# A transformer step on one core: token sums on VectorE, Strassen's products in another order, and norms moved and shared between ScalarE and VectorE

## The chip, the core and the metric

The kernel runs on one core of one Trainium2 chip. A core has a matrix engine (TensorE, PE in the profile; its weight loads are PEld), a vector engine (VectorE, DVE), a scalar engine (ScalarE, ACT), a general engine (GpSimd, POOL) and a queue that issues transfers (SyncE, SP). Each engine takes its own instructions in order and waits on semaphores for the others. [...] The metric is the time of one execution in microseconds (us) on the device; lower is better.

## The reference, cut to what matters

One layer of a hybrid backbone: a context pass over 128 tokens (`x_prompt`) and a denoising step over 1024 tokens (`x_sample`), width 1024. The change touches its last part, the feed-forward block and the norm behind it, and the place where the first norm hands over to it:

```python
h = x * (1 + sc2) + sh2
ff = jnp.square(jax.nn.relu(h @ w_up)) @ w_down      # 1024 -> 4096 -> 1024
x = layer_norm(ALPHA * x + g2 * ff, ln2_g, ln2_b)    # mean and variance of each token's row

def layer_norm(x, g, b):
    mu = jnp.mean(xf, -1, keepdims=True)
    var = jnp.mean(jnp.square(xf - mu), -1, keepdims=True)
    return ((xf - mu) * lax.rsqrt(var + EPS)) * g + b
```

`sc2`, `sh2` and `g2` come from the conditioning vector and differ between the two groups of tokens. All in float32.

## The kernel before

The 1152 tokens are nine blocks of 128, numbered 0 to 8 (8 is the prompt), in three groups of 384: (0, 1, 2), (3, 4, 5), (6, 7, 8). Every product of 32-bit numbers is made as three matmuls: each operand is split into a rounded part (`hi`, written by ACT, line 72) and the remainder (`lo`, a subtraction on DVE, line 73), and hi x hi, hi x lo and lo x hi are added up in PSUM (`mm3`, or line 1366 for the halves below). Weights come as `raw` tiles of 128 x 1024 by DMA on SP's queue (two such tiles), and are split into `wh` and `wl` (four of each).

The instructions are put in order by a planner of the language, not by the text alone: what stands earlier in the text goes first among what is ready by the planner's own clock, and what is ready can be drawn far ahead of its place. The order that comes out is fixed per engine at build time. Tiles of one tag share a number of slots; a tile that finds none waits until an older one is released.

The first norm (lines 1080 to 1100) takes the blocks in the order 0, 1, 2, 6, 7, 8, 3, 4, 5. Behind it the feed-forward block runs in two parts.

*First 384 tokens* (`T0`). Sixteen rounds, one per 256 of the 4096 inner columns: `up_plain` makes the relu squared of 2 x 128 inner rows, `down_bank` adds their part of the output into six PSUM banks that stay (`dacc`). Beside these rounds `act_forms` makes, for the other 768 tokens, the sums and differences that Strassen's method needs: for each of four slices, four sums hi + lo (line 1119), then four differences (line 1125), each split into hi and lo again. They stand in the rounds as a generator of which `some_forms` takes two steps at a time. After the last round `out0` computes per block g2 x sum + ALPHA x residual, the row's statistics and the norm, and stores it.

*Other 768 tokens* (`T1`, blocks 3 to 8). Again sixteen rounds. `up_halves` makes 256 inner rows for two halves of 384 tokens with seven products instead of eight (line 1366), each of 12 matmuls over 384 columns, on combinations of the weights (`up_forms`: four sums and differences on POOL, line 1283, and seven splits into three slots `uf`) and of the tokens (`acts`). The products are added up in PSUM banks x, y and z in the order

```python
ORDER = ("a11", "s2", "s1", "s3", "s4", "a12", "a22")
BANK = "xyzyzxy"
```

and the four results, (row half, token half) = (1,1), (0,1), (0,0) and (1,0) in that order, pass through `half_out` (relu, square, split). A bank that is added to a second time must have been read before. `down` then adds the round's part of the output: for each of six blocks and two halves of 512 columns six matmuls into one of five `d` banks and one DVE add into `acc` (line 1168). One round of `up_halves` is ahead of `down`.

*End.* Before the last `down`, which takes two rounds at once, `residual` turns `acc` into g2 x acc + ALPHA x residual for all six blocks: a product on POOL (line 1130) and two additions on DVE (line 1135) with the residual's halves loaded into tiles `x` (two slots). In the last `down`, DVE multiplies each bank by g2 (line 1171), adds it (line 1172) and takes the row's statistics (line 1173); `ln_stats` makes mean, variance and 1/sqrt (two small steps on POOL, lines 1050 and 1051); `finish` subtracts the mean on ACT (line 1145), multiplies by 1/sqrt and gain on DVE (line 1146), adds the bias on POOL (line 1147; DVE for the last block, in two halves) and stores.

Of the kernel before, what the change touches and what calls it, by code (L numbers as in the profile page):

```python
# [15 lines left out]
D = 1024  # L16
# [20 lines left out]
def hybrid_step_kernel(  # L37
# [1042 lines left out]
    for i, s in enumerate(SORD):  # L1080
# [4 lines left out]
        for half in range(2):  # L1085
# [5 lines left out]
            mm3(g[:], terms)  # L1091
            cs = slice(512 * half, 512 * half + 512)
# [17 lines left out]
    def act_forms(mk):  # L1110
# [4 lines left out]
        for k in range(4):  # L1115
            full = []
            for nm in ("a11", "s1", "a12", "s4"):
                t = mk([128, TB], "v" + nm)
                nc.gpsimd.tensor_tensor(out=t[:], in0=f(acts[nm][0][:, k, :]), in1=f(acts[nm][1][:, k, :]), op=ALU.add)
                full.append(t)  # L1120
                yield
            b11, b12, b21, b22 = full
            t3 = mk([128, TB], "vs3")
            for dst, x, y, nm in ((t3, b22, b12, "s3"), (b11, b12, b11, "s1"), (b22, b22, b11, "s2"), (b21, b21, b22, "a22")):
                nc.gpsimd.tensor_tensor(out=dst[:], in0=x[:], in1=y[:], op=ALU.subtract)
                split(acts[nm][0][:, k, :], acts[nm][1][:, k, :], dst[:])
                yield

    def residual(mk, acc_s, s, g2):
        nc.gpsimd.tensor_tensor(out=acc_s, in0=acc_s, in1=g2, op=ALU.mult)  # L1130
# [6 lines left out]
    def finish(mk, acc_s, s, l2, mv, rs, n):  # L1137
        out = y_sample[0, 128 * s:128 * s + 128, :] if s < NS else y_prompt[0]
        nmu = mk([128, 1], "nmu", 2)
        nc.vector.tensor_scalar(nmu[:], mv[:, 0:1], -1.0, None, ALU.mult)  # L1140
        w = D // n
        for i in range(n):
            cs = slice(w * i, w * i + w)
            y = acc_s[:, cs]
            nc.scalar.activation(out=y, in_=y, func=AF.Identity, bias=nmu[:])  # L1145
            nc.vector.scalar_tensor_tensor(out=y, in0=y, scalar=rs[:], in1=l2[0][:, cs], op0=ALU.mult, op1=ALU.mult)  # L1146
            (nc.gpsimd if n == 1 else nc.vector).tensor_tensor(out=y, in0=y, in1=l2[1][:, cs], op=ALU.add)
            store(out[:, cs], y)

# [3 lines left out]
    def down(mk, acc, toks, fbs, parts, ws, g2, l2, split_last):  # L1153
        last = g2 is not None
        ws = [(parts[i // 2], i % 2, w) for i, w in enumerate(ws)]
        fin = None
        for i, s in enumerate(toks):
            ts_ = slice(128 * i, 128 * i + 128)
            if last:
                st = mk([128, 2, 6], "bst", 2)  # L1160
            for half in range(2):
                cs = slice(512 * half, 512 * half + 512)
                g = psd.tile([128, 512], F32, tag="d", bufs=5, name="d4")
                mm3(g[:], [((a[0][:, m, ts_], a[1][:, m, ts_]), (w[0][:, 0, cs], w[1][:, 0, cs])) for a, m, w in ws])
                if fbs[0] == 0:
                    nc.vector.tensor_copy(out=acc[:, i, cs], in_=g[:])
                elif not last:
                    nc.vector.tensor_tensor(out=acc[:, i, cs], in0=acc[:, i, cs], in1=g[:], op=ALU.add)  # L1168
                else:
                    tm = mk([128, 512], "x", 2)  # L1170
                    nc.vector.tensor_tensor(out=tm[:], in0=g[:], in1=g2[0 if s < NS else 1][:, cs], op=ALU.mult)  # L1171
                    nc.vector.tensor_tensor(out=acc[:, i, cs], in0=acc[:, i, cs], in1=tm[:], op=ALU.add)  # L1172
                    nc.vector.bn_stats(out=st[:, half, :], in_=acc[:, i, cs])  # L1173
            if last:
                if fin:
                    finish(mk, *fin, 1)
                fin = (acc[:, i, :], s, l2, *ln_stats(st, mk))
        if last:
            finish(mk, *fin, 2 if split_last else 1)
# [12 lines left out]
    def up_plain(fb, each):  # L1192
        w = w_pair(w_up, 256 * fb)
# [46 lines left out]
    def some_forms():  # L1240
        next(forms, None)
        next(forms, None)
# [21 lines left out]
    ORDER = ("a11", "s2", "s1", "s3", "s4", "a12", "a22")  # L1264
    BANK = "xyzyzxy"
# [4 lines left out]
    def up_forms(fb):  # L1270
# [24 lines left out]
        yield form(a11)  # L1295
        yield form(s2)
# [5 lines left out]
        yield form(a12)  # L1302
        yield form(a22)
# [4 lines left out]

    def out0(s):
        y = fft([128, D], "y0", 3)  # L1310
        st = fft([128, 2, 6], "bst", 2)
        for half in range(2):
# [3 lines left out]
            nc.vector.tensor_tensor(out=y[:, cs], in0=dacc[s][half][:], in1=g2a[:, cs], op=ALU.mult)  # L1316
            nc.vector.scalar_tensor_tensor(out=y[:, cs], in0=x1[:], scalar=ALPHA, in1=y[:, cs], op0=ALU.mult, op1=ALU.add)
            nc.vector.bn_stats(out=st[:, half, :], in_=y[:, cs])
        finish(fft, y, s, l2a, *ln_stats(st, fft), 1)
# [4 lines left out]
    down_bank(NFB - 1, nxt, ws[1], out0)  # L1324
    s4f.close()
# [6 lines left out]
    ar = pool(st4, "ar", 1)  # L1332
    acc = ar.tile([128, 6, D], F32, name="acc")

# [4 lines left out]
    
# [6 lines left out]
    def up_halves(pre, a, each):  # L1346
# [3 lines left out]
        def tmp(nm):  # L1350
            u[nm] = ft([128, 512], "x", 2)[:, 0:TB] if nm == "v" else ft([128, TB], nm)[:]
# [5 lines left out]
        for j, nm in enumerate(ORDER):  # L1357
            fresh = BANK[j] not in bank
            if fresh:
                bank[BANK[j]] = (psd.tile([128, 512], F32, tag="z", name="pz") if BANK[j] == "z" else  # L1360
# [109 lines left out]
```

## Time and profile before

| | |
|---|---|
| time, median of 3 runs | 2481.15 us (2478.34 to 2482.4) |
| the profiled execution's own time | 2481.37 us |
| its span in the trace | 2479.6 us |
| first norm with the output product, blocks 0 to 8 | 1545 to 1654 us |
| first 384 tokens | 1654 to 1944 us |
| other 768 tokens | 1944 to 2461 us (last matmul) |
| last matmul to the end | 18.4 us |

The profile is that of one execution. Its views give the busy time of each engine by stretch, groups of equal instructions with count, busy time, mean ns of one and the idle time of their engine just ahead of them, the waits of one engine for another, the chain that ended last, and the instructions in order of time (start, length, engine, line, operation, output and inputs, and in brackets the idle time before with what ended it). `L73` is line 73 of the kernel; a helper such as `split` has one line for all its uses, so its groups go by the names of the tiles. A matmul's end is modelled. PE's granted clock is given as a share of full speed.

### The profile page before, as it was taken

How to read it: one execution, taken by the hardware profiler on the slowest of the kernel's cores; microseconds unless marked ns; L12 is line 12 of the kernel's file. 1: busy time of each engine (PE TensorE's matmuls, PEld its weight loads, DVE VectorE, ACT ScalarE, POOL GpSimd, SP SyncE). 2: the span in 40 equal slices, each digit the busy share in tenths (PEclk: the TensorE clock that was granted, in tenths of full speed). 3: DMA queues.
4: the chain of work that ended last, by engine and by line, in shares of the span. 5: the costliest groups of instructions: out<-in, count | busy, mean ns of one | idle time of the engine just before them, and what ended most of it. 6: DMA issues, size and time to landing. Idle time of an engine off the chain costs nothing. (4 is left out here: it accounts for less than half of the span.)

```text
span 2479.6 us, 35982 instructions
## 1 busy us (share of the span) xinstructions
PE 2371.1 (96%) x13293; PEld 2141.3 (86%) x13293; DVE 1492.7 (60%) x2695; ACT 989.7 (40%) x2100; POOL 481.6 (19%) x632
## 2 busy tenths in 40 slices
PE   7999998999999899899999999998999899999996
PEld 4878887788899899889999999887999799999985
DVE  5645635646654464378787346676444666666678
ACT  3323423534433243166666323124333444444432
POOL 1001100211111010144442000236000422222243
PEclk9999999999999999999999999998999999999998
DMA  8275547445655652520002665333443322222223
GB/s 269 83 203 153 149 116 198 136 126 153 193 160 150 173 154 90 106 69 16 16 16 71 207 187 187 101 127 123 141 129 120 114 77 69 68 69 69 69 82 110
DMA packets 234544, 300.46 MB, mean 121 GB/s; under 512 B 24992, under 2 KB 175600, under 8 KB 234368
## 3 DMA queue, kind: packets, MB, share of 16 engines
q1 hardware_dynamic: 234368, 298.16, 39.9%
q8 instruction: 105, 1.72, 0.3%
q14 instruction: 71, 0.58, 0.1%
HBM read 232.88 MB, written 65.21 MB: 120 GB/s over the span
## 5 line engine op out<-in xcount | busy, mean ns | idle before, releaser
L78 PE MATMUL g<-th,wh 128*128 128x384 f32 x1088 | 373.5, 343 | 8.8 <-DVE fm L248 8.8
L80 PE MATMUL g<-th,wl 128*128 128x384 f32 x1088 | 368.3, 338 | 0.0
L79 PE MATMUL g<-tl,wh 128*128 128x384 f32 x1088 | 366.5, 337 | 0.0
L73 DVE TENSOR_TENSOR wl<-raw,wh 128x1024 fp32r<-128x1024 f32 x180 | 226.5, 1265 | 134.6 <-ACT wh L72 133.8
L72 ACT ACTIVATE wh<-raw 128x1024 fp32r<-128x1024 f32 x180 | 188.9, 1058 | 258.2 <-DMA raw<-in_w_down_dram 90.9
L78 PE MATMUL g<-wh,th 128*128 128x512 f32 x600 | 241.1, 402 | 0.3 <-DVE mmt L266 0.2
L80 PE MATMUL g<-wh,tl 128*128 128x512 f32 x600 | 236.2, 394 | 0.0
L79 PE MATMUL g<-wl,th 128*128 128x512 f32 x600 | 236.0, 394 | 0.3 <-DVE wl L73 0.3
L78 PEld LDWEIGHTS g<-th,wh 128*128 128x128 f32 x1088 | 206.5, 190 | 17.6 <-DVE fm L248 9.1
L79 PEld LDWEIGHTS g<-tl,wh 128*128 128x128 f32 x1088 | 206.4, 190 | 0.1
L80 PEld LDWEIGHTS g<-th,wl 128*128 128x128 f32 x1088 | 206.0, 189 | 0.4 <-issue 0.4
L78 PEld LDWEIGHTS g<-wh,th 128*128 128x128 f32 x600 | 113.2, 189 | 25.7 <-issue 3.8
L80 PEld LDWEIGHTS g<-wh,tl 128*128 128x128 f32 x600 | 113.0, 188 | 23.3
L79 PEld LDWEIGHTS g<-wl,th 128*128 128x128 f32 x600 | 113.2, 189 | 21.2 <-DVE wl L73 1.4
L72 ACT ACTIVATE ph<-t 128x384 fp32r<-128x384 f32 x192 | 90.9, 493 | 70.9 <-PE t L872 70.4
L1168 DVE TENSOR_TENSOR acc<-acc,d 128x512 f32<-128x512 f32 x156 | 101.9, 681 | 28.5 <-PE d L80 28.4
L248 DVE COPY fm<-g 128x384 f32<-128x384 f32 x96 | 53.2, 554 | 101.0 <-PE g L80 100.3
L73 DVE TENSOR_TENSOR pl<-t,ph 128x384 fp32r<-128x384 f32 x192 | 104.7, 548 | 9.1 <-ACT ph L72 7.1
L1283 POOL TENSOR_TENSOR wtl<-raw 128x512 f32<-128x512 f32 x16 | 20.9, 1304 | 438.3 <-PE pa L79 211.3
L872 PE MATMUL t<-ident,pe 128*128 128x128 f32 x576 | 96.1, 276 | 6.2 <-DVE pl L73 5.2
L78 PE MATMUL u<-th,wh 128*128 128x384 f32 x256 | 89.6, 350 | 10.9 <-ACT wh L72 7.2
L80 PE MATMUL u<-th,wl 128*128 128x384 f32 x256 | 89.0, 348 | 1.8 <-DVE wl L73 1.8
(386 smaller groups left out, 6002.8 us busy)
## 6 DMA issues: line engine op xcount, KB each, us to landing
raw<-in_w_up_dram SPq DMA_DIRECT2D x64, 512.0 KB
raw<-in_w_down_dram SPq DMA_DIRECT2D x64, 512.0 KB
raw<-in_w_in_dram SPq DMA_DIRECT2D x44, 512.0 KB
kvt<-kvd SPq DMA_DIRECT2D x64, 257.0 KB
raw<-in_w_mod_dram SPq DMA_DIRECT2D x32, 512.0 KB
kvd<-kvs SPq DMA_DIRECT2D x36, 257.0 KB
uw<-ud SPq DMA_DIRECT2D x72, 128.0 KB
bs<-st SPq DMA_DIRECT2D x32, 258.0 KB
```

The costliest lines, as they stand in the source:

```text
L72: nc.scalar.activation(out=hi, in_=src, func=AF.Copy)
L73: nc.vector.tensor_tensor(out=lo, in0=src, in1=f(hi), op=ALU.subtract)
L78: nc.tensor.matmul(out, lhsT=ah, rhs=bh, start=start and i == 0, stop=False)
L79: nc.tensor.matmul(out, lhsT=ah, rhs=bl, start=False, stop=False)
L80: nc.tensor.matmul(out, lhsT=al, rhs=bh, start=False, stop=stop and i == n - 1)
L248: nc.vector.tensor_copy(out=st[:], in_=g[:, 0:TB])
L872: nc.tensor.transpose(pt[:, k, :], pexp[u][:, kt * 128:kt * 128 + 128], ident[:])
L1168: nc.vector.tensor_tensor(out=acc[:, i, cs], in0=acc[:, i, cs], in1=g[:], op=ALU.add)
L1283: nc.gpsimd.tensor_tensor(out=tmp[i], in0=x, in1=y, op=op)
```

## The change

Five things, all behind line 1089:

1. The first weights of `up_plain` are asked for within the last block of the first norm.
2. The token sums and differences of `act_forms`, and the g2 product in `residual` and the bias add in `finish`, are made by DVE instead of POOL. The generator has fewer steps (six per slice instead of eight), and `some_forms` takes one at a time.
3. The seven products run in another order, with four accumulating banks x, y, p and z; `d` has four banks instead of five. The sum for (1,1) moves from POOL to DVE, and (1,0) is made from a22's copy `w`.
4. After the last `down_bank` of the first 384 tokens only g2 x bank is taken; residual, statistics, norm and store follow in the text after the first `up_halves` of the other tokens. The pool of `acc` is opened behind them.
5. At the end two blocks (3 and 4, `LATE`) take their g2 product and residual in the last `down`, behind their banks. Row statistics of all blocks but the last are made by ACT (three passes, two of them with a running sum) with three small steps on POOL; the last block keeps those of DVE.

```diff
@@ first norm @@
             mm3(g[:], terms)
+            if s == SORD[-1] and half == 0:
+                wup0 = w_pair(w_up, 0)
@@ act_forms @@
-            for nm in ("a11", "s1", "a12", "s4"):
+            for i, nm in enumerate(("a11", "s1", "a12", "s4")):
                 t = mk([128, TB], "v" + nm)
-                nc.gpsimd.tensor_tensor(out=t[:], in0=f(acts[nm][0][:, k, :]), in1=f(acts[nm][1][:, k, :]), op=ALU.add)
+                nc.vector.tensor_tensor(out=t[:], in0=f(acts[nm][0][:, k, :]), in1=f(acts[nm][1][:, k, :]), op=ALU.add)
                 full.append(t)
-                yield
+                if i % 2:
+                    yield
...
-                nc.gpsimd.tensor_tensor(out=dst[:], in0=x[:], in1=y[:], op=ALU.subtract)
+                nc.vector.tensor_tensor(out=dst[:], in0=x[:], in1=y[:], op=ALU.subtract)
@@ residual @@
-        nc.gpsimd.tensor_tensor(out=acc_s, in0=acc_s, in1=g2, op=ALU.mult)
+        nc.vector.tensor_tensor(out=acc_s, in0=acc_s, in1=g2, op=ALU.mult)
@@ finish @@
-            nc.scalar.activation(out=y, in_=y, func=AF.Identity, bias=nmu[:])
+            if not centred:
+                nc.scalar.activation(out=y, in_=y, func=AF.Identity, bias=nmu[:])
             nc.vector.scalar_tensor_tensor(out=y, in0=y, scalar=rs[:], in1=l2[0][:, cs], op0=ALU.mult, op1=ALU.mult)
-            (nc.gpsimd if n == 1 else nc.vector).tensor_tensor(out=y, in0=y, in1=l2[1][:, cs], op=ALU.add)
+            nc.vector.tensor_tensor(out=y, in0=y, in1=l2[1][:, cs], op=ALU.add)
...
+    def stats_act(mk, y, jk):
+        sm, nmu, ss, rs = (mk([128, 1], nm, 2) for nm in ("sm", "nmu", "sq", "brs"))
+        nc.scalar.activation(out=jk, in_=y, func=AF.Copy, accum_out=sm[:])
+        nc.gpsimd.tensor_scalar(nmu[:], sm[:], -1.0 / D, None, ALU.mult)
+        nc.scalar.activation(out=y, in_=y, func=AF.Identity, bias=nmu[:])
+        nc.scalar.activation(out=jk, in_=y, func=AF.Square, accum_out=ss[:])
+        nc.gpsimd.tensor_scalar(rs[:], ss[:], 1.0 / D, EPS, ALU.mult, ALU.add)
+        nc.gpsimd.tensor_tensor(out=rs[:], in0=rs[:], in1=mhalf[:, 0:1], op=ALU.pow)
+        return nmu, rs, True
@@ down @@
-                g = psd.tile([128, 512], F32, tag="d", bufs=5, name="d4")
+                g = psd.tile([128, 512], F32, tag="d", bufs=4, name="d4")
...
-                elif not last:
-                    nc.vector.tensor_tensor(out=acc[:, i, cs], in0=acc[:, i, cs], in1=g[:], op=ALU.add)
+                elif not last or s in late:
+                    nc.vector.tensor_tensor(out=y[:, cs], in0=y[:, cs], in1=g[:], op=ALU.add)
...
+                if s in late:
+                    residual(mk, y, s, gs)
                 if fin:
                     finish(mk, *fin, 1)
-                fin = (acc[:, i, :], s, l2, *ln_stats(st, mk))
+                fin = (y, s, l2, *(stats_dve(mk, st) if end else stats_act(mk, y, jk)))
@@ products @@
-    ORDER = ("a11", "s2", "s1", "s3", "s4", "a12", "a22")
-    BANK = "xyzyzxy"
+    ORDER = ("a11", "a22", "a12", "s2", "s1", "s3", "s4")
+    BANK = "xyxpzpz"
@@ norm of the first 384 tokens @@
+    def out0_bank(s):
+        for half in range(2):
+            cs = slice(512 * half, 512 * half + 512)
+            nc.vector.tensor_tensor(out=y0[s][:, cs], in0=dacc[s][half][:], in1=g2a[:, cs], op=ALU.mult)
...
-    down_bank(NFB - 1, nxt, ws[1], out0)
-    s4f.close()
+    down_bank(NFB - 1, nxt, ws[1], out0_bank)
@@ up_halves @@
+            if j in (0, 1, 4):
+                nc.scalar.activation(out=tmp({0: "u1", 1: "w", 4: "v"}[j]), in_=o, func=AF.Copy)
+            elif j == 2:
+                half_out(a, 0, 0, o)
+            elif j == 3:
+                tsum(tmp("u2"), u["u1"], o)
+            elif j == 5:
+                tsum(u["u1"], u["u1"], o)
+                tsum(u["v"], u["u1"], u["v"])
+                half_out(a, 1, 1, u["v"])
+                tsum(u["w"], u["u1"], u["w"])
+                half_out(a, 1, 0, u["w"])
+            else:
+                tsum(u["u2"], u["u2"], o)
+                half_out(a, 0, 1, u["u2"])
@@ rounds of the other 768 tokens @@
     a = up_halves(pre, aa[0], lambda: None)
     pre = up_begin(1)
+    for s in T0:
+        out0(s)
+    s4f.close()
+    ar = pool(st4, "ar", 1)
+    acc = ar.tile([128, 6, D], F32, name="acc")
...
-    todo = list(enumerate(T1))
+    g2b = [ft([128, D], f"g2{g}") for g in range(2)]
+    for g in range(2):
+        load(g2b[g][:], gmod[1, g, :].partition_broadcast(128))
+    todo = list(enumerate(T1))[2:]
```

More of the change, by code (lines that the diff above doesn't have):

```diff
@@ L1144, in finish, with stats_dve, down @@
             y = acc_s[:, cs]
-            nc.scalar.activation(out=y, in_=y, func=AF.Identity, bias=nmu[:])
+            if not centred:
+                nc.scalar.activation(out=y, in_=y, func=AF.Identity, bias=nmu[:])
             nc.vector.scalar_tensor_tensor(out=y, in0=y, scalar=rs[:], in1=l2[0][:, cs], op0=ALU.mult, op1=ALU.mult)
-            (nc.gpsimd if n == 1 else nc.vector).tensor_tensor(out=y, in0=y, in1=l2[1][:, cs], op=ALU.add)
+            nc.vector.tensor_tensor(out=y, in0=y, in1=l2[1][:, cs], op=ALU.add)
             store(out[:, cs], y)
+    def stats_dve(mk, st):
+        mv, rs = ln_stats(st, mk)
+        nmu = mk([128, 1], "nmu", 2)
+        nc.vector.tensor_scalar(nmu[:], mv[:, 0:1], -1.0, None, ALU.mult)
+        return nmu, rs, False
+    def stats_act(mk, y, jk):
[7 more added lines that the diff above has]
+        return nmu, rs, True
     def down_w(fbs):
         return [wslot([(0, wdv[:, 2 * fb + m:2 * fb + m + 1, :])], 1024) for fb in fbs for m in range(2)]
-    def down(mk, acc, toks, fbs, parts, ws, g2, l2, split_last):
+    def down(mk, acc, toks, fbs, parts, ws, g2, l2, late):
         last = g2 is not None
+        jk = l2 and l2[2]
         ws = [(parts[i // 2], i % 2, w) for i, w in enumerate(ws)]
@@ L1158, in down @@
             ts_ = slice(128 * i, 128 * i + 128)
-            if last:
+            y, gs = acc[:, i, :], g2 and g2[0 if s < NS else 1]
+            end = i + 1 == len(toks)
+            if last and end:
                 st = mk([128, 2, 6], "bst", 2)
@@ L1192, in up_plain @@
     def up_plain(fb, each):
-        w = w_pair(w_up, 256 * fb)
+        w = w_pair(w_up, 256 * fb) if fb else wup0
         ah = fat([128, 2, TB], "ah", 2, F32R)
@@ L1241, in some_forms @@
         next(forms, None)
-        next(forms, None)
     for fb in range(NFB - 2):
@@ L1295, in up_forms @@
         yield form(a11)
+        yield form(a22)
+        yield form(a12)
         yield form(s2)
@@ L1301, in up_forms @@
         yield form(s4)
-        yield form(a12)
-        yield form(a22)
     def up_begin(fb):
@@ L1315, in out0 @@
             load(x1[:], x1d[s][:, cs])
[L1316 to L1319, printed above, removed]
+            y = y0[s][:, cs]
+            nc.vector.scalar_tensor_tensor(out=y, in0=x1[:], scalar=ALPHA, in1=y, op0=ALU.mult, op1=ALU.add)
+            nc.vector.bn_stats(out=st[:, half, :], in_=y)
+        finish(fft, y0[s], s, l2a, *stats_dve(fft, st), 1)
     ws = [down_w([fb]) for fb in (NFB - 2, NFB - 1)]
```

61 lines of the change are left out of this document (19 added, 42 removed).

## The prediction

> **What bounds the kernel now.** The page's busy shares first, then busy time by stretch; the stretches are cut where PE's work changes (columns: length, then busy time and count of PE, PEld, DVE, ACT and POOL, granted PE clock, DMA share, GB/s).
>
> ```profile
> PE 2371.1 (96%) x13293; PEld 2141.3 (86%) x13293; DVE 1492.7 (60%) x2695; ACT 989.7 (40%) x2100; POOL 481.6 (19%) x632
> 1545.00:1654.30 109.30, 109.30 (x519) 91.89 (x519) 72.89 (x118) 24.12 (x42) 31.52 (x24) 1.00 0.31 106
> 1654.30:1736.90 82.60, 69.66 (x318) 62.10 (x317) 58.46 (x65) 33.07 (x55) 46.21 (x35) 0.86 0.41 134
> 1736.90:1927.10 190.20, 190.20 (x973) 174.32 (x972) 80.93 (x93) 70.81 (x93) 0.00 (x0) 1.00 0.42 130
> 1943.50:1971.70 28.20, 18.15 (x85) 17.00 (x83) 24.92 (x37) 10.52 (x19) 14.59 (x12) 0.82 0.33 115
> 2002.80:2374.00 371.20, 371.20 (x1871) 336.79 (x1871) 250.14 (x348) 154.94 (x276) 83.06 (x60) 1.00 0.22 69
> 2389.20:2407.90 18.70, 16.90 (x73) 13.34 (x72) 15.08 (x18) 5.76 (x9) 12.04 (x6) 1.00 0.28 84
> 2407.90:2425.40 17.50, 15.48 (x86) 14.48 (x85) 14.06 (x18) 7.42 (x14) 9.87 (x4) 1.00 0.34 113
> 2425.40:2461.20 35.80, 33.39 (x145) 26.66 (x143) 30.61 (x50) 6.92 (x10) 9.34 (x9) 1.00 0.27 92
> 2461.20:2479.60 18.40, 0.00 (x0) 0.00 (x0) 14.94 (x20) 3.58 (x4) 10.02 (x9) 0.64 0.28 114
> ```
>
> PE is the bound: where it is fed (1736.9 to 1927.1, 2002.8 to 2374) it is busy all the time at clock 1.00, so no engine's saving counts there. PE's number of products is not changed. What can be won lies in four stretches: around the token sums (1654 to 1737), at the start of the last 768 tokens (1943 to 1972), around the last rounds (2389 to 2461), and the tail without PE (18.4 us).
>
> What PE's work costs undisturbed, from the chain of waits in a middle round (start, length, what):
>
> ```profile
> 2127.11 4.18 PE u L1366 x24
> 2137.55 4.16 PE u L1366 x24
> 2158.07 4.18 PE u L1366 x24
> ```
>
> Seven products take 2137.55 + 4.16 - 2127.11 = 14.6 us; twelve down banks take 2158.07 - 2141.71 = 16.4, or 1.36 a bank. Losses against that: 1654 to 1737 holds 318 records, at 190.20/973 us each 62.2, so **20.4 us** lost. 1943.5 to 1971.7 holds seven products: 28.2 - 14.6 = **13.6**. The last rounds: 18.7 - 16.4, 17.5 - 14.6 and 35.8 - 2 x 16.4 make **8.2**. With the tail, 60.6 us lie within the change's reach. Idle alone is less than this: the clock of 0.86 and 0.82 says that PE also runs slowly after a stop.
>
> Who makes PE wait, from the waits of PE after 1440 us (total, times, longest), then two rows of ACT's timeline, the groups of the sums, and the same DVE operation alone and beside POOL:
>
> ```profile
> PE u L1366 <- ACT uf L72: 7.5, 1, 7.5
> PE u L78 <- ACT wh L72: 7.2, 2, 5.9
> PE u L78 <- ACT r L1200: 3.7, 1, 3.7
> 1709.71 0.52 ACT L72 ACTIVATE tfs3h<-vs 128x384 fp32r<-128x384 f32 x1 [2.90 <-POOL vs L1125]
> 1710.14 1.04 ACT L72 ACTIVATE wh<-raw 128x1024 fp32r<-128x1024 f32 x1
> L1119 POOL TENSOR_TENSOR va<-th,tl x8: 1029/1336/2000, 1685.4 to 1718.8; 128x384 f32<-128x384 f32 x8
> L1125 POOL TENSOR_TENSOR vs<-vs,vs x4: 1011/1250/1876, 1657.4 to 1717.6; 128x384 f32<-128x384 f32 x4
> L73 DVE TENSOR_TENSOR tl<-m,th 128x384 fp32r<-128x384 f32 x16 | 8.9, 556 | 6.4 <-ACT th L72 6.3
> L73 DVE TENSOR_TENSOR tfs2l<-vs,tfs2h 128x384 fp32r<-128x384 f32 x4 | 5.0, 1239 | 0.3 <-ACT tfs2h L72 0.3
> L73 DVE TENSOR_TENSOR tfa22l<-va,tfa22h 128x384 fp32r<-128x384 f32 x4 | 3.6, 905 | 1.8 <-ACT tfa22h L72 1.8
> ```
>
> ACT takes its queue in order. The weight copy that PE needs (1710.14) stands behind the rounding of a sum that POOL has not made, and DVE beside POOL needs 0.91 to 1.24 us for 0.56 us of work. The rows' starts also show that the order of issue is not that of the text: sums written into eight rounds all run before 1723.
>
> **Token sums on DVE.** 16 sums and 16 differences leave POOL (32 x about 1.3 = 42 us) and cost DVE 32 x 0.556 = 17.8 us. DVE was busy 58.5 of 82.6 us there, and gives back what POOL cost it: 16 remainders x some 0.5 = 8. It fits, and cover beyond 1737 is ample (80.9 of 190.2 busy); without it 17.8 us would be added. Gone are the 7.2 us wait on `wh` and most of the slow clock after it. Left is the 3.7 us wait on `r` (behind the last layer norm, whose own POOL product stays) with its slow stretch, 5 us in all: gain **15**. Bounds: 3, if DVE's queue blocks ACT as POOL did; 20, if all goes. The earlier first up weights (`wup0`) move two loads and two splits ahead of the last tokens; PE is busy all of 1545 to 1654 as it is, so 0, within 1 either way.
>
> **Norm of the first 384 tokens later.** Before, three whole norms stood in ACT's and DVE's queues ahead of the new weights:
>
> ```profile
> 1955.66 1.15 ACT L1145 ACTIVATE y<-y,nmu 128x1024 f32<-128x1024 f32 x1 [4.12 <-DVE nmu L1140]
> 1956.71 0.61 ACT L72 ACTIVATE uf<-raw 128x512 fp32r<-128x512 f32 x1
> L1048 DVE BATCH_NORM_AGGREGATE bmv<-bst 128x2 f32<-128x12 f32 x18 | 3.6, 200 | 0.1
> L1140 DVE TENSOR_SCALAR nmu<-bmv 128x1 f32<-128x1 f32 x9 | 1.3, 143 | 0.0
> L1318 DVE BATCH_NORM_STATS2 bst<-y 128x6 f32<-128x512 f32 x6 | 4.1, 682 | 0.0
> L1146 DVE SCALAR_TENSOR_TENSOR y<-y,brs,l2a 128x1024 f32<-128x1024 f32 x3 | 3.8, 1280 | 0.7 <-ACT y L1145 0.7
> L1061 DVE TENSOR_TENSOR m<-m 128x1024 f32<-128x1024 f32 x9 | 11.0, 1225 | 20.9 <-POOL m L1060 20.9
> L1168 DVE TENSOR_TENSOR acc<-acc,d 128x512 f32<-128x512 f32 x156 | 101.9, 681 | 28.5 <-PE d L80 28.4
> ```
>
> Now only six products with g2 (6 x 0.68 = 4.1 us) free the banks; the 7.5 us wait goes. What remains per token is 4 x 0.68 + 0.34 + 1.28 + an add of 1.23 that was POOL's: 5.6, or 16.7 us for three, inside the next rounds. There DVE has, per seven products, 7 x 0.68 weight remainders, 5 x 0.56 sums, 4 x 0.56 and 2 x 1.23 remainders (by the rows of equal width): 12.3 of 14.6 us. Two such sets take 24.6 of 29.2, so 12 us of the norms are left over; the down round behind has 16.4 - 12 x 0.68 = 8.2 free. Some 4 us fall on PE, and I add 2 for order. A wait is added: `acc` now takes its room only when the norms' stores have landed, and behind its first copy on DVE stand eleven more, then PE at the fifth bank. The x1 loads share two slots with `v` and `w`; behind a late `w` copy on ACT stand the weight copies. On SP the three stores and six x1 loads now stand among the rounds' weight loads, and a store that waits for DVE holds those; a round's weights have the whole round before to arrive, so 0 here and part of the lower bound. The two loads of g2 go behind the loop and are needed last. Loss 6 instead of 13.6: gain **7.6**, bounds -2 (all serial) and 13.6.
>
> **Products in another order.** PE's 84 matmuls are the same. POOL loses its 16 sums, DVE gains one (0.56 us), ACT one copy, in rounds with a third of DVE free. The first three weight forms need no POOL difference any more. New is that the third product needs the first one's copy; before, s1 and s4 had that distance on bank z without a stall in the middle rounds. The price is the banks: `d` has four instead of five. A first add that ends more than 3 x 1.36 = 4.1 us after its bank stops PE. From DVE's timeline:
>
> ```profile
> 2144.27 1.92 DVE L73 TENSOR_TENSOR uf<-wth,uf 128x512 fp32r<-128x512 f32 x2
> 2146.12 0.67 DVE L1168 TENSOR_TENSOR acc<-acc,d 128x512 f32<-128x512 f32 x1
> ```
>
> The first bank ends at 2141.71 + 1.36 = 2143.07, its add at 2146.79: 3.7 late, just inside. Ahead of the adds DVE will have four sums, three remainders and three weight remainders, 2.2 + 1.7 + 2.1 = 6.0 us, against 6.6 now (with POOL's slowing). I take 0.15 us a round, **-2** for 14; bounds 0 and -15.
>
> **The end.** POOL's products and adds slow DVE most here:
>
> ```profile
> 2446.15 2.40 POOL L1147 TENSOR_TENSOR acc<-acc,l 128x1024 f32<-128x1024 f32 x1 [2.31 <-DVE acc L1146]
> 2446.59 2.50 DVE L1172 TENSOR_TENSOR acc<-acc,x 128x512 f32<-128x512 f32 x1
> L1172 DVE TENSOR_TENSOR acc<-acc,x 128x512 f32<-128x512 f32 x12 | 12.7, 1068 | 0.0
> L1130 POOL TENSOR_TENSOR acc<-acc,g 128x1024 f32<-128x1024 f32 x6 | 16.5, 2761 | 7.7 <-DVE acc L1168 7.7
> 2475.20 1.28 DVE L1147 TENSOR_TENSOR acc<-acc,l 128x512 f32<-128x512 f32 x2
> L1050 POOL TENSOR_SCALAR brs<-bmv 128x1 f32<-128x1 f32 x18 | 5.3, 294 | 294.7 <-DVE bmv L1048 294.4
> L1051 POOL TENSOR_TENSOR brs<-brs,mhalf 128x1 f32<-128x1 f32 x18 | 10.6, 588 | 1.5
> ```
>
> DVE takes six products with g2 (6 x 1.23) and five last adds (5 x 1.23), 13.5 us; it loses ten statistics (6.8) and the slowing of 12 x 0.4 = 4.6 in L1172 alone. Two residuals move behind the last banks, so the down rounds start with less ahead of them. Per token DVE then has 5.2 us (6.5 for the two late ones) against PE's 5.5: level with PE, where now 14.9 us of DVE's work are left when PE ends. Of the stalls (2.3, 2.9, 3.0) I leave 0, 2 (x1 loads and `v` share slots) and 1.5 (the half `(1,0)` is ready sooner, but behind another): 3.5 instead of 8.2. The tail: three operations on the last half 2.0, aggregate 0.3, `rs` 0.9, four half operations 2.7, 1.6 left of the token before, then 2479.6 - 2476.5 = 3.1 for the store: 10.6 instead of 18.4. Gain 4.7 + 7.8 = **12.5**, bounds 3 (DVE sums to as much as before) and 17. ACT's three passes per token (3 x 1.15) end some 5 us behind the adds and have nothing of PE behind them.
>
> The three small POOL steps of a token's statistics stand beside a DVE that is full; by the means of L1050 and L1051, 0.29 and 0.59, the 0.9 above is all they cost. [...]
>
> **Sum.** 15 + 7.6 - 2 + 12.5 = 33 off the profiled execution's 2481.4 (span 2479.6), which is 0.2 above the median shown: **2448**.
>
> **Rivals.** *Four banks too few (slower).* If sums and remainders of three halves stand ahead of the adds with their ACT waits, the first add ends later than 4.1 us; each us more costs 14. It decides from 35/14 = 2.5 us a round; at 3 us 2481.4 - 35 + 42 = 2488. For it: 3.7 is close to 4.1. Against: DVE's sum there does not grow. Chance 0.07. *Short stops lower the clock (slower).* Stops at every bank bring the 0.82 of 1943 into each down round: 14 x 16.4 x (1/0.82 - 1) = 50, 2498. [...] Here 2389 to 2408, with stops, kept 1.00. Chance 0.02. *DVE's queue blocks ACT like POOL's*: the first gain is 3, 2460; for it, DVE would be near full in that stretch; 0.12. *The norms' stop only moves* (DVE overfull, `acc` waits): second gain 0, 2456; 0.12. *The tail stays*, DVE having 13.5 us more: end gain 4, 2457; 0.09. Two of these at once or a lesser bank stall: 2465 to 2478, 0.08. Nearly all losses gone (20, 12 and 15 us won, no bank stall): 2434 to 2440, 0.05. My forecast, 2441 to 2455: 0.45.
>
> **Numbers.** What a measurement of this kernel can tell from no change is about 0.2%, 5 us. Faster: 0.45 + 0.12 + 0.12 + 0.09 + 0.05 and half of the pairs, 0.87; same 0.04; slower 0.09. The range 2434 to 2470 leaves out the two slower cases and half the pairs.
>
> **What would show it.** The stretch of 1654: no ACT row `[<-POOL vs]`, clock near 1.00. At 1943: no `uf` wait over 2 us. Rounds of 30.96 us still 30.96: if longer by over 1 us with PE `d` waiting on DVE `acc`, the banks were too few and the forecast is wrong. From last matmul to end: 10 to 11 us.

## The result and the profile after

The changed kernel takes 2462.98 us (median of four runs, 2459.17 to 2465.72), the kernel before 2480.33 beside it (four runs, 2478.34 to 2482.4): a ratio of 0.9929, with a 95% interval of 0.9912 to 0.9946. That is 17.4 us, where the forecast was 2448 and 33. The profiled execution took 2459.17 (span 2457.4), so like stands against like in the traces: 2479.6 of span before, 2457.4 after.

The same view as in the prediction, busy time by stretch, of the changed kernel (columns: length, then busy time and count of PE, PEld, DVE, ACT and POOL, granted PE clock, DMA share, GB/s); the stretches are cut at the same pieces of work, and the third and the last rounds are cut again where something stops:

```profile
1652.70:1718.00 65.30, 61.89 (x318) 56.81 (x317) 57.42 (x98) 33.28 (x56) 4.05 (x3) 0.97 0.45 141
1718.00:1924.60 206.60, 206.60 (x1046) 187.85 (x1045) 88.68 (x104) 73.56 (x99) 8.79 (x7) 1.00 0.41 132
1979.60:2382.40 402.80, 402.55 (x2028) 365.11 (x2026) 283.70 (x396) 168.49 (x313) 74.54 (x52) 1.00 0.23 71
2382.40:2403.30 20.90, 20.87 (x109) 19.08 (x107) 13.11 (x18) 6.98 (x12) 0.00 (x0) 1.00 0.38 127
2403.30:2414.50 11.20, 4.16 (x13) 4.17 (x14) 2.97 (x5) 3.08 (x7) 0.00 (x0) 0.63 0.28 93
2414.50:2440.00 25.50, 25.50 (x109) 20.64 (x107) 21.83 (x29) 14.80 (x22) 4.94 (x10) 0.96 0.17 62
2440.00:2457.40 17.40, 0.00 (x1) 0.00 (x0) 12.42 (x18) 5.38 (x9) 2.88 (x7) 0.61 0.30 121
```

Read the first row against the prediction's row for 1654.30 to 1736.90: the same 318 records of PE, 65.3 us in place of 82.6, clock 0.97 in place of 0.86. The token sums have given what was hoped. The middle rounds (third row) are 13 in 402.8 us, 30.98 each, as before. Then comes something new: 11.2 us in which PE is busy for 4.2, at clock 0.63, and behind it a tail of 17.4 us, where 18.4 had been and 10.6 was forecast.

In which pieces the time went, worked out from the first and last matmuls of the same pieces in both traces (us):

| Piece | Before | After | Won | Forecast |
|---|---|---|---|---|
| last `g` matmul to the end of the third `down_bank` | 82.4 | 65.3 | 17.2 | 15 |
| first product of the last 768 tokens to start of their third `up_halves` | 59.4 | 55.1 | 4.3 | 7.6 |
| from there to the last `up_halves` | 405.1 | 402.8 | 2.3 | 2.3, less 2 for the banks |
| last `up_halves` to last matmul | 53.2 | 57.6 | -4.4 | 2.4 |
| last matmul to end | 18.4 | 17.4 | 1.0 | 7.8 |

Two matmuls of the changed kernel's third `up_halves` run 15 us ahead of the others and are left out of the count. The rest of the 22 us of span is the work before the change's first place (the last `g` matmul ends at 1652.76 and not at 1654.46). That end lies anywhere from 1648.7 to 1655.2 in the fourteen profiles of this study, though the work in front of it hardly differs, so below pieces are compared, and not only spans.

Who makes PE wait, in the waits of PE of the changed kernel, between 1640 and 1740, between 1920 and 1980 and from 2380 on (total, times, longest):

```profile
PE u L78 <- ACT r L1224: 2.4, 1, 2.4
PE u L195 <- ACT r L1224: 1.0, 1, 1.0
PE pp L1390 <- ACT y L1147: 4.7, 1, 4.7
PE pz L1390 <- ACT x L1393: 7.1, 1, 7.1
```

Two stops are left: one of 4.7 us behind a norm's centring on ACT at 1951, one of 7.1 us at 2403 behind a mere copy out of PSUM, where PE's sums lie. To see why the copy is late, follow it to ACT's timeline and to DVE's (start, length, engine, line, operation, idle time before it and what ended it):

```profile
2391.31 0.51 ACT L72 ACTIVATE ab<-r 128x384 fp32r<-128x384 f32 x1
2409.79 0.49 ACT L1393 ACTIVATE x<-pz 128x384 f32<-128x384 f32 x1 [17.97 <-DVE acc L1138]
```

```profile
2395.61 0.69 DVE L1138 SCALAR_TENSOR_TENSOR acc<-x,acc 128x512 f32<-128x512 f32 x1 [1.82 <-DMA x<-x1d]
...
2399.01 0.69 DVE L1138 SCALAR_TENSOR_TENSOR acc<-x,acc 128x512 f32<-128x512 f32 x1 [1.65 <-DMA x<-x1d]
2402.45 0.69 DVE L1138 SCALAR_TENSOR_TENSOR acc<-x,acc 128x512 f32<-128x512 f32 x1 [2.75 <-DMA x<-x1d]
2405.70 0.69 DVE L1138 SCALAR_TENSOR_TENSOR acc<-x,acc 128x512 f32<-128x512 f32 x1 [2.56 <-DMA x<-x1d]
2409.02 0.69 DVE L1138 SCALAR_TENSOR_TENSOR acc<-x,acc 128x512 f32<-128x512 f32 x1 [2.62 <-DMA x<-x1d]
```

ACT stands still for 18 us, not because it has work but because the copy of `v` needs one of the two `x` slots. `w` took the other at 2387 and holds it until `v` exists. Two of the residuals' eight halves of x1 had passed before that, at 2377 and 2378; the other six pass one after another through a single slot: load, 0.69 us on DVE, load again, the last four of them one in 3.3 us. PE waits for the bank, ACT for the slot, DVE for the DMA. What looks like "PE waits for ACT" is a shortage of room.

### The profile page after: what moved, and what is told of

It reads as the page before. It is cut to its first block, busy times and chain, and to the rows that moved or that the text cites. A ratio compares the mean times of both kernels' runs of the same rounds, so it can differ in the third digit from the quotient of the medians.

```text
span 2457.4 us, 35978 instructions
## 1 busy us (share of the span) xinstructions
PE 2360.4 (96%) x13293; PEld 2133.9 (87%) x13293; DVE 1489.1 (61%) x2733; ACT 1002.8 (41%) x2136; POOL 387.7 (16%) x575
## 4 chain that ended last, share of the span: by engine, by line
PE 82%; DVE 6%; DMA 6%; ACT 2%; issue 2%; POOL 1%; SPq 0%; DVEq 0%; ACTq 0%; POOLq 0%
PE g L78 13%; PE g L80 12%; PE g L79 12%; PE u L1390 4%; PE d L78 3%; PE d L79 3%; PE d L80 3%; PE pz L1390 2%; PE pp L1390 2%; PE t L872 2%; PE pa L79 2%; PE pa L80 2%; PE pa L78 2%; PE u L78 2%; PE u L80 2%
## 5 line engine op out<-in xcount | busy, mean ns | idle before, releaser
L78 PEld LDWEIGHTS g<-th,wh 128*128 128x128 f32 x1088 | 205.8, 189 | 18.1 <-DVE fm L248 9.6
L1189 DVE TENSOR_TENSOR acc<-acc,d 128x512 f32<-128x512 f32 x160 | 109.9, 687 | 62.9 <-PE d L80 61.0
L861 POOL TENSOR_SCALAR pe<-pe,rs 128x1152 f32<-128x1152 f32 x64 | 79.0, 1234 | 54.8 <-DVE rs L860 27.0
```

The source lines that it names most:

```text
L78: nc.tensor.matmul(out, lhsT=ah, rhs=bh, start=start and i == 0, stop=False)
L861: nc.gpsimd.tensor_scalar(pe[:], pe[:], rs[:, 0:1], 1.0, ALU.mult, ALU.mult)
L1189: nc.vector.tensor_tensor(out=y[:, cs], in0=y[:, cs], in1=g[:], op=ALU.add)
```

## The experiments

The theory on trial: the sums on DVE gave their whole gain; what is missing is lost because x1 shares two slots with `v` and `w`, in the residuals at the end and in the norms of the first 384 tokens. The rival: DVE, which took over 13.5 us of POOL's work, is the bound at the end, and without the stop the tail is longer by as much. Every ratio is to the kernel before, run beside it.

| Run | Ratio (95% interval) | Last `g` to last `pa` | to last matmul | Tail |
|---|---|---|---|---|
| before | 1 | 289.2 | 517.5 | 18.4 |
| changed | 0.9929 (0.9912 to 0.9946) | 272.0 | 515.3 | 17.4 |
| e1 residuals' own room | 0.9876 (0.9859 to 0.9892) | 271.9 | 508.1 | 15.4 |
| e2 early rows' own room | 0.9901 (0.9886 to 0.9916) | 272.6 | 511.6 | 17.6 |
| e3 both | 0.9862 (0.9847 to 0.9877) | 271.9 | 503.9 | 15.7 |
| e4 both, norms in round 0 | 0.9878 (0.9863 to 0.9893) | 272.0 | 510.1 | 15.3 |
| e5 sums on POOL | 0.9981 (0.9970 to 0.9992) | 286.6 | 515.4 | 17.4 |
| e6 before, sums on DVE | 0.9937 (0.9924 to 0.9949) | 271.9 | 517.6 | 17.0 |
| e7 before, four banks | 1.0034 (1.0021 to 1.0047) | 286.8 | 526.2 | 17.0 |
| e8 e3, no late residual | 0.9882 (0.9865 to 0.9898) | 271.8 | 501.9 | 15.9 |
| e9 e3, statistics on DVE | 0.9859 (0.9841 to 0.9877) | 273.2 | 502.6 | 16.1 |
| e10 e3, bias on POOL | 0.9888 (0.9868 to 0.9907) | 271.8 | 503.6 | 21.4 |
| e11 e8, bias on POOL | 0.9866 (0.9851 to 0.9881) | 271.6 | 502.8 | 20.5 |
| e12 e9, bias on POOL | 0.9880 (0.9862 to 0.9897) | 272.0 | 502.2 | 18.1 |

The last three columns are of the one profiled execution, in us.

**e1, room for the residuals.** The row goes into a weight slot, which is free between two rounds' weights:

```diff
-            residual(ft, acc[:, i, :], s, g2b[0 if s < NS else 1][:])
+            row = f(wp.tile([128, 1024], F32R, tag="w" + "hl"[i % 2], name="x1w")[:])
+            residual(ft, acc[:, i, :], s, g2b[0 if s < NS else 1][:], row)
...
+        if row is not None:
+            load(row, x1d[s][:])
```

> The changed kernel, with one thing other: the four residuals that are due during the last up_halves read their x1 row whole (128x1024) into a weight slot that is free then, and no longer by halves into the two x slots that v and w also use. Theory (the x slots are what the end lost): the 18 us wait of the copy of pz into x on DVE L1138 and the 7 us gap of the matmuls before the last rounds go; about 9 us of the matmuls' time with the slower clock behind the gap, and some 4 us more of the tail, since DVE starts into the last additions with nothing left over: 2463 becomes about 2450 (2447 to 2454). Rival (DVE's own work after the last additions begin, 38 us from the first to the end, is the bound): the gap goes, the last matmul comes 9 us earlier, and the tail grows by as much: 2460 to 2464.

Measured 2447.55 us beside 2477.17, 0.53% below the changed kernel's ratio, or 13 us. The wait of 7.1 us is gone; PE's waits from 2380 on are now

```profile
PE d L79 <- DVE wl L73: 0.7, 1, 0.7
PE d L78 <- ACT wh L72: 0.5, 1, 0.5
```

and the last matmul comes 7.1 us earlier, counted from the last `pa` (8.2 earlier, counted from the start of the last `up_halves`: 49.4 us for 57.6); the tail is 2.0 us shorter. The rival said that the tail would grow. The theory stands, with the tail's share smaller than I had put it (4).

**e2, room for the early rows.** The norms of the first 384 tokens read x1 whole into two weight rows and one gate row that are free by then:

```diff
-            x1 = fft([128, 512], "x", 2)
-            load(x1[:], x1d[s][:, cs])
+        x1 = fft([128, D], "g20") if s == 0 else fft([128, D], "raw", 2)
+        load(x1[:], x1d[s][:])
```

> The changed kernel, with one thing other: the norms of the first 384 tokens read their x1 rows whole into slots that are free by then (two of the weight rows of the first round, one of the gate row), and no longer by halves into the two x slots. Theory (the loads could only start when v and w had left the slots, at 1939 us, and threw the norms into the second round): DVE does most of the norm work between 1926 and 1941 us, where it was idle; the gap of 4.6 us at 1951 us and the slow matmuls behind it go: the first two rounds of the last 768 tokens lose 4 to 5 us of their 9.5, 2463 becomes 2458 to 2459. Rival (ACT's centring, which waits for DVE's mean with the copies of v and w behind it, is in the way wherever the norms stand): the gap moves into the first round, 2462 to 2465.

2453.66 us, ratio 0.9901. The piece from the last `pa` to the last matmul is 3.7 us shorter than in the changed kernel, close to the 4 to 5 expected; of that 2.7 lie at the edited place (52.3 us for 55.1 from the first product of these tokens to their third `up_halves`) and 1.0 at the end, which the edit doesn't touch. The span is 6.9 us shorter (2450.5), but 4.1 of that lie ahead of the edited place (last `g` at 1648.7) and are scatter. **e3** makes both edits:

> The changed kernel with the x1 rows of both places in room of their own (the two edits before together). Theory: the two gains lie at different times and add: 2463 becomes 2445 (2442 to 2450). Rival (DVE bounds the end, ACT's centring the start): 2460 to 2465.

2444.65 us, ratio 0.9862. The gains add: 3.7 from e2 and 9.1 from e1 (7.1, and 2.0 of tail) make 12.8, and e3 is 13.2 below the changed kernel in the same columns. By the ratios the gains of e1, e2 and e3 are 13.1, 6.9 and 16.6 us, each some 3.5 more; the changed kernel's own ratio, to which all three are compared, is known to within 4 us, so the pieces are the better measure. The waits of PE there between 1920 and 1980 show the large stop gone and smaller ones in its place:

```profile
PE pp L1395 <- DVE u L1384: 2.0, 1, 2.0
PE d L78 <- DVE acc L1192: 1.3, 2, 0.7
PE pz L1395 <- DVE uf L73: 0.6, 1, 0.6
```

**e4, the norms inside the first round.**

```diff
-    a = up_halves(pre, aa[0], lambda: None)
-    pre = up_begin(1)
-    for s in T0:
-        out0(s)
+    rows = iter((None, None, 0, None, 1, None, 2))
...
+    a = up_halves(pre, aa[0], out0_next)
+    pre = up_begin(1)
```

> As the kernel before this one, and the three norms of the first 384 tokens are emitted inside the first round of the last 768 tokens, one each after products 2, 4 and 6. If the place in the program still decides when the norms run, this gains another 2 to 4 us against it (2441 to 2444); if the free slots alone let them run in DVE's idle time, it is the same within 1 us; if ACT's centring in that round stands before copies that the products wait for, it loses 2 to 5 us (2447 to 2450).

2448.81 us, ratio 0.9878: 4 us more than e3, which the intervals don't tell apart, but the piece to the last matmul is 6.2 longer, and nearly all of that lies at the edited place (57.9 us for 52.0 from the first product to the third `up_halves`). The third answer, but on another engine: PE waits for DVE, whose queue now has norm steps ahead of a weight remainder (waits of PE in 1920 to 1980, then DVE's timeline):

```profile
PE u L1395 <- DVE uf L73: 5.0, 1, 5.0
PE pp L1395 <- DVE nmu L1160: 2.1, 1, 2.1
```

```profile
1941.38 1.27 DVE L1153 SCALAR_TENSOR_TENSOR y<-y,brs,l2a 128x1024 f32<-128x1024 f32 x1
1942.58 0.55 DVE L1384 TENSOR_TENSOR x<-u,x 128x384 f32<-128x384 f32 x1
1943.05 1.22 DVE L1154 TENSOR_TENSOR y<-y,l2a 128x1024 f32<-128x1024 f32 x1
...
1945.36 1.88 DVE L73 TENSOR_TENSOR uf<-raw,uf 128x512 fp32r<-128x512 f32 x3
```

So of the two places tried for the three norms the change has the better one; what they lacked was room for their loads.

**e5 and e6, the sums.** e5 is the changed kernel with `nc.gpsimd` in the two lines of `act_forms`, e6 the kernel before with `nc.vector` there and nothing else:

```diff
-                nc.vector.tensor_tensor(out=t[:], in0=f(acts[nm][0][:, k, :]), in1=f(acts[nm][1][:, k, :]), op=ALU.add)
+                nc.gpsimd.tensor_tensor(out=t[:], in0=f(acts[nm][0][:, k, :]), in1=f(acts[nm][1][:, k, :]), op=ALU.add)
```

> The changed kernel with the token sums on POOL again, as before the change (28 additions and subtractions with their splits; their order in the program and the earlier load of the first up weights stay). Theory (POOL's sums held the splits on ACT and through them the matmuls): 15 to 18 us are lost between 1654 and 1740 us, with ACT waiting for POOL's vs tiles; 2463 becomes 2478 to 2481. Rival (the earlier weights, or one sum a step in place of two, brought that gain): 2463 to 2468.

> The kernel before with one thing other: the token sums on DVE. Theory: it gains by itself the 15 to 18 us of the stretch from 1654 to 1740 us, 2480 becomes 2462 to 2465, as fast as the whole change, so that all else in the change brings next to nothing (as it stands, with the x slots shared). Rival (it needs the earlier weights and the later norms too): a gain of 5 us or less, 2475 or more.

(The edit moves 32 additions and subtractions, eight for each of four slices, and not 28.) e5: 2472.9 us beside 2477.21, ratio 0.9981, 0.52% or 12.9 us above the changed kernel; its piece is 14.6 us longer; both are under the 15 to 18 expected and far from the rival's 0 to 5. The old waits are back, of PE and of ACT from 1650 to 1740:

```profile
PE u L78 <- ACT wh L72: 7.3, 2, 5.9
```

```profile
ACT tfs3h L72 <- POOL vs L1128: 8.1, 3, 4.8
ACT tfa22h L72 <- POOL va L1128: 7.3, 4, 2.4
```

e6: 2461.39 us, ratio 0.9937, with the piece at 271.9 as in the changed kernel. Neither the earlier weights nor the pace of one step for two has a share. And e6 alone is, within the intervals, as fast as the whole change (0.9937 and 0.9929): everything else in it came to about nothing as it stood.

**e7, four banks in the old order** (`bufs=4` for 5 in `down`, nothing else):

> The kernel before with one thing other: four d banks in place of five. Theory (DVE takes a bank within about 2 us of its last matmul in the rounds of 30.96 us, so the fifth is idle): 2480 becomes 2479 to 2482, rounds of 30.96 stay. Rival (four are too few where DVE is behind, in the first and the last rounds): up to 17 us are lost in down's first and last calls, 2485 to 2497; by my own rhythm of before it was worth at most that.

2485.22 us, ratio 1.0034, slower by 8.4 us. The theory, that the fifth bank was idle before as well, is wrong. The piece to the last matmul is 8.7 us longer, not in the first and last rounds alone, as the rival had it: each of thirteen rounds is longer than its like before, most by 0.1 to 0.4 us. Of PE's waits (1990 to 2480, those of over 0.15 us alone) one has grown:

```profile
PE d L78 <- DVE acc L1168: 5.0, 6, 2.1
```

In the kernel before, that wait is 1.8 us; the rest of the loss is not in the list. The traces say why the bank is missed. From the end of a bank's last matmul to the end of DVE's addition the first three banks of a middle round took 3.6, 3.3 and 4.0 us (medians), up to 5.4, where a bank comes every 1.36 us; with the new order of products they take 0.7, 0.7 and 1.6, and no more in any middle round. In the kernel before, three of POOL's weight sums run from 2140.6 to 2145.0, beside the remainders that DVE makes ahead of the first addition at 2146.1; in the changed kernel the same sums are done at 2144.9, and the first bank ends at 2150.3. So the new order seems to pay for the bank that it takes. This is read from the timelines: no run has the new order with five banks, or the old one with its sum on DVE.

**e8, no late residual.** e3 with all six residuals during the last `up_halves`:

```diff
-    LATE = T1[:2]
+    LATE = ()
-    todo = list(enumerate(T1))[2:]
+    todo = list(enumerate(T1))
```

> The kernel with both x1 rooms, and no residual left for the last additions: all six are done during the last up_halves, each with its row in a weight slot. Theory (the tail of 15.6 us there is DVE's backlog, to which the two late residuals give 2 x (1.23 + 1.29) = 5 us after the last additions begin): the tail becomes 10 to 12 us, 2445 becomes 2440 to 2442. Rival (the five us only move into up_halves, where DVE has about 4 us idle from 2380 to 2402, and the last weights' splits on ACT and DVE come later by as much, with a gap of the matmuls): 2444 to 2449.

2445.89 us, ratio 0.9882, not told apart from e3. The tail is 15.9 us: 5 us less for DVE in the last stretch has not shortened it at all. So it is not simply DVE's backlog. The waits of DVE from 2398 on:

```profile
DVE acc L1153 <- POOL brs L1170: 4.5, 5, 1.1
DVE x L1197 <- PE d L80: 1.3, 2, 0.8
DVE acc L1153 <- POOL brs L1051: 0.9, 1, 0.9
```

DVE waits 4.5 us, at every token, for the 1/deviation that comes from ACT's three passes by way of POOL. **e9** takes that wait away (e3 with `bn_stats` on DVE for all six tokens):

```diff
-                    if end:
-                        nc.vector.bn_stats(out=st[:, half, :], in_=y[:, cs])
+                    nc.vector.bn_stats(out=st[:, half, :], in_=y[:, cs])
...
-                fin = (y, s, l2, *(stats_dve(mk, st) if end else stats_act(mk, y, jk)))
+                fin = (y, s, l2, *stats_dve(mk, st))
```

> The kernel with both x1 rooms (2445 us), and the row sums of the last six tokens' norms all on DVE's statistics again, where ACT had five of them by three passes of its own. Theory (DVE is the bound from 2400 us on: about 4.8 us of its work for a token of 4.67 us of matmuls, and then waits of 0.5 to 1.4 us for the 1/deviation that comes late from ACT's passes by way of POOL): DVE gets 5 x 2 x 0.6 = 6 us more, and loses 3.7 us of waits: 2445 becomes 2446 to 2449, the tail 16 to 19 us. Rival (ACT's passes are what DVE waits for, and the sharing is no help): 2439 to 2443.

(The 4.67 us in it is a slip: a token has 24 matmuls at 0.23, 5.5 us.) 2446.14 us, ratio 0.9859, e3's within the interval, and a tail of 16.1 us, as the theory had it. The waits are gone, and their place is taken by work. The last down rounds of e3, then of e9, by stretch:

```profile
2398.30:2428.50 30.20, 30.13 (x131) 24.43 (x131) 24.23 (x31) 16.41 (x25) 4.82 (x12) 1.00 0.18 70
2428.50:2444.10 15.60, 0.00 (x0) 0.00 (x0) 11.17 (x16) 3.63 (x5) 2.61 (x5) 0.58 0.25 101
```

```profile
2401.20:2429.40 28.20, 28.16 (x125) 22.98 (x123) 27.76 (x46) 4.62 (x4) 3.18 (x8) 1.00 0.19 75
2429.40:2445.40 16.00, 0.00 (x0) 0.00 (x0) 12.00 (x20) 2.48 (x3) 1.58 (x4) 0.61 0.25 99
```

In e9 DVE is busy for 27.76 of 28.2 us; in e3 for 24.23 of 30.2, and waits in the rest. The tail is the same. Sharing the row norms between ACT and DVE has so far brought nothing that can be measured.

**e10, e11, e12, the bias addition on POOL**, as before the change, in e3, in e8 and in e9 (in e12 the condition reads `n == 1 and s >= 3`, which takes the same five tokens):

```diff
-            nc.vector.tensor_tensor(out=y, in0=y, in1=l2[1][:, cs], op=ALU.add)
+            (nc.gpsimd if centred else nc.vector).tensor_tensor(out=y, in0=y, in1=l2[1][:, cs], op=ALU.add)
```

> The kernel with both x1 rooms, and the addition of the norm's bias for five of the last six tokens on POOL again, as before the change. Theory (DVE bound): DVE loses 5 x 1.14 = 5.7 us of work, of which 3 to 5 us come off the tail of 15.6: 2440 to 2442. Rival (POOL's addition, 2.73 us in the profile of before, stands ahead of the small steps from which ACT centres and DVE scales the next token): their waits grow by as much as DVE saves, 2444 to 2449.

> The same on the kernel that has no late residual either (2446 us). Theory (DVE bound, 5 us less for DVE before the last additions and 5.7 us less in them): 2437 to 2440. Rival (POOL's queue): 2443 to 2449.

> The kernel of e9 (both x1 rooms, all statistics on DVE, 2446 us), and the bias addition of five of the last six tokens on POOL, which has only two small steps a token there. Theory (DVE, busy for 28.9 of the 30 us from 2398 to 2428 us and without a wait in them, bounds the end): 5 x 1.14 = 5.7 us less for it bring the end 4 to 6 us earlier, 2440 to 2442, the tail 10 to 12 us. Rival (DVE's scaling now waits for 1/deviation behind POOL's additions of 2.7 us, as it did before the change): 2445 to 2450.

2453.25, 2447.2 and 2447.91 us. No tail is shorter: 21.4, 20.5 and 18.1 us. The rivals were right that it brings nothing, but POOL's queue is only a part of why (in e10, DVE's waits for `brs` grow from 4.9 to 8.0 us). In e12 DVE has five additions of 1.21 us less and is as full as in e9 (27.7 of the last 28.2 us with matmuls in both), since its other work gets longer. The groups of e9, then those of e12, with the same operations:

```profile
L1198 DVE TENSOR_TENSOR acc<-acc,x 128x512 f32<-128x512 f32 x8 | 5.3, 679 | 0.0
L1197 DVE TENSOR_TENSOR x<-d,g 128x512 f32<-128x512 f32 x8 | 5.2, 659 | 0.0
L1143 DVE SCALAR_TENSOR_TENSOR acc<-x,acc 128x512 f32<-128x512 f32 x4 | 2.6, 686 | 0.0
```

```profile
L1198 DVE TENSOR_TENSOR acc<-acc,x 128x512 f32<-128x512 f32 x8 | 9.0, 1151 | 0.0
L1197 DVE TENSOR_TENSOR x<-d,g 128x512 f32<-128x512 f32 x8 | 5.2, 652 | 0.0
L1143 DVE SCALAR_TENSOR_TENSOR acc<-x,acc 128x512 f32<-128x512 f32 x4 | 4.8, 1236 | 0.0
```

and how a single one lies beside POOL's addition, by POOL's and by DVE's timeline:

```profile
2431.11 2.35 POOL L1154 TENSOR_TENSOR acc<-acc,l 128x1024 f32<-128x1024 f32 x1 [2.03 <-DVE acc L1153]
```

```profile
2431.73 2.27 DVE L1198 TENSOR_TENSOR acc<-acc,x 128x512 f32<-128x512 f32 x1
```

DVE's addition ends at 2434.00, after POOL's at 2433.46. In all, 3.7 + 2.2 = 5.9 us of stretching against 5 x 1.21 = 6.1 saved, and DVE's wait for the last `brs` is 1.5 us longer (2.4 for 0.9).

## Why the prediction was right and wrong

The direction was right. The time, 2463, lies above the 2441 to 2455 that I called my forecast, and only the wide range of 2434 to 2470 holds it. In the traces the pieces won 20.4 us where my terms add up to 33.1: 2.2 more at the token sums and 2.0 more at the banks, 3.3 less at the norms, 13.6 less at the end. None of my rivals gave this sum; that the errors partly cancel is luck.

**The token sums: right.** Forecast 15, measured 17.2 in the piece of the changed kernel, and 14.6 and 17.3 in e5 and e6 (e7, with the same work there as the kernel before, has 286.8 for its 289.2, so more than a range isn't to be had). No row of ACT there waits for POOL's `vs`, the clock is 0.97, and DVE got back what POOL had cost it: the remainder that took 1239 ns in the prediction's rows takes 552 (changed kernel, 1650 to 1740):

```profile
L73 DVE TENSOR_TENSOR tfs2l<-vs,tfs2h 128x384 fp32r<-128x384 f32 x4 | 2.2, 552 | 0.0
```

What I left as lost, the wait on `r`, is there with 2.4 and 1.0 us. The lower bound (DVE's queue blocking ACT) did not come: ACT waits 5.6 us in all for DVE's sums there, and none of it reaches PE.

**The norms of the first 384 tokens: right mechanism, a term too small.** Forecast was a loss of 6, measured 9.3, so 4.3 won of 7.6. The step was "some 4 us fall on PE, and I add 2 for order"; the shared slots were named in the same part but had no price of their own. e2 and e3 give that price, 2.7 and 3.1 us in this piece. Without it the loss is 6.2 to 6.6, near the forecast's 6, and in e3 PE's stops there are behind DVE (2.0, 1.3 and 0.6), where I had put some 4 us.

**Products in another order and four banks: the sum harmless, the reasoning mis-sized.** I put 2 us of loss, from a DVE that has 6.0 us ahead of the first addition in place of 6.6. The rounds stayed at 30.98 us, so 0; but the lag of the first addition did not shrink a little, it went from 3.6 to 0.7. "Just inside", which I said of 3.7 against 4.1, was wrong even for the old order, as e7 shows: there four banks cost 8.4 us, with a third bank that is taken 4.0 us late in the median and up to 5.4. The rival of too few banks is real there, and does not come with the change's order.

**The end: the failed step.** Forecast 12.5, measured -1.1 (the last three rows of the table of pieces: 2.3, -4.4 and 1.0). Two terms:

- "2 (x1 loads and `v` share slots)": the stop cost 7.1 us, and the next twelve matmuls took 4.21 in place of 2.25 at the lower clock (0.63 from 2403.3 to 2414.5), and the five behind them 2.1 in place of 1.1: 10 in all. I had the mechanism and not its count: six half rows pass one slot, some 3.3 us each, as long as the slot of `w` is held. e1 takes it out: the piece from the last `up_halves` to the last matmul is 8.2 shorter (two stops of 0.7 and 0.5 are left), the tail 2.0.
- The tail of 10.6. It was 17.4, and 15.3 to 16.1 without the stop (e1, e3, e4, e8 and e9). "Level with PE", 5.2 us of DVE's work a token against PE's 5.5, left out the waits: DVE's scaling of a token stands for 0.5 to 1.4 us until the 1/deviation is there. In e3 that is 3.7 us, and DVE begins the product of the last half 4.1 us after the last matmul, where I had it at once. That the waits make this delay is read from the timeline; no run takes them out without adding work. The other items of my list are near what was measured (in e3: the last half 1.9 for 2.0, `brs` 1.2 for 0.9, the token before 2.3 for 1.6, the store 3.1). e9 shows that the wait can't be traded for DVE's own statistics, e8 that it isn't the late residuals.

Of the rivals, the tail that stays was the one that came, though not as I had put it: I had priced it with 4 us won at the end, and its reason, DVE's 13.5 us of added work, is not borne out as it stands: e8 has 5 us less of it in the last stretch, and the same tail as e3. The clock did not fall in the rounds: 1.00 from 1979.6 to 2382.4, and 0.63 from 2403.3 to 2414.5, around the stop of 7.1 us.

For the small POOL steps I had taken the rows' price. On the last chain that was near: the last wait for `brs` is 0.9 us in the changed kernel and 1.2 in e3, with DVE idle beside it. Beside a working DVE it is not. In e3 the same `nmu` step takes 0.22 us at one token and 1.05 at another, where it begins 0.3 us into DVE's scaling of a token and ends 0.1 us after it (POOL's timeline, then DVE's):

```profile
2424.71 0.22 POOL L1166 TENSOR_SCALAR nmu<-sm 128x1 f32<-128x1 f32 x1 [3.25 <-ACT l L1165]
2428.57 1.05 POOL L1166 TENSOR_SCALAR nmu<-sm 128x1 f32<-128x1 f32 x1 [0.35 <-ACT l L1165]
```

```profile
2428.26 1.28 DVE L1153 SCALAR_TENSOR_TENSOR acc<-acc,brs,l 128x1024 f32<-128x1024 f32 x1 [1.09 <-POOL brs L1170]
```

Two of the five `nmu` steps of e3's last tokens are longer so: ACT waits 1.18 and 1.17 us for them, and 0.34 to 0.37 for the other three. So POOL's step was slowed beside DVE, as DVE's addition was beside POOL.

What stays open: whether the scaling of a token, put one token later in DVE's order, would end the waits without added work, and bring the tail to the 10.6 us that the sum of its steps gives. It wasn't tried. e3, e9 and e11 have the lowest ratios, 0.986 to 0.987 of the kernel before, up to twice the change's gain; e1, e4, e8 and e12, at 0.988, are not told apart from them.

## What to carry to other kernels

Before moving a load behind other work, count who holds the room that it lands in and how often it must be filled: a wait of PE for a copy was in truth a slot through which six loads had to pass one by one. An order of work can pay for a resource given up beside it, so try the resource alone on the old order before calling it spare. And work given to POOL may not be off DVE: in e12 five additions saved it 6.1 us, and its own operations beside them that read two operands from SBUF (where the kernel keeps its tiles, but for PE's sums) took 5.9 us more; compare the mean of the same operation with and without it.

## What the runs showed of the hardware

How much DVE's operations slowed beside POOL went with their operands in these traces. In e12, of the operations that lie with over half of their length beside one of POOL, those that read both inputs from SBUF took 1.31 us on average (`acc<-acc,x`, six, up to 2.27) against 0.67 alone, and 1.79 against 0.69 (`acc<-x,acc`, two). Those with one input in PSUM (`x<-d,g`, seven) took 0.65 against 0.67, and the statistics with one input (`bst<-acc`, three) 0.68 in both cases. In the kernel before, other operations of the token sums' stretch show the same: `r<-r` 1.36 against 0.55 (two beside POOL), `wl<-raw,wh` 1.73 against 1.22 (seven, from 1650 to 1740). One group seems not to fit: `uf<-raw,uf` in the middle rounds, two inputs in SBUF, 0.69 in both cases (thirteen beside POOL). But there DVE began 0.2 us before POOL every time, and it is POOL's sum that is long: 1.35 us each (`x<-r,x`), where sums of the same size took 1.00 us at the least in the stretch of the token sums. In row 2431.73 of e12 DVE begins 0.62 us into POOL's 2.35 and ends at 2434.00, after POOL's end at 2433.46. In the `nmu` step of e3 at 2428.57 the roles are exchanged: POOL begins 0.31 us into DVE's 1.28 and ends at 2429.62, after DVE's end at 2429.54.

A stop of 7.1 us cost some 3 us more than itself: the twelve matmuls behind it took 4.21 us, those of the same product in the rounds 2.25, and the next five took 2.1 in place of 1.1. The clock was 0.63 over the stretch from the stop to the end of those twelve.
